# The end of a decoder layer: the last columns in two groups of 256, their squares on VectorE, scalings and transfers shared out anew

## The chip, the cores and the metric

One core of one Trainium2 chip runs the whole layer. The metric is the device time of one execution in microseconds (us), the median over several runs. Engines are named as the profile names them: PE is TensorE (PEld its weight loads), DVE is VectorE, ACT is ScalarE, POOL is GpSimd, and SP (SPq) is SyncE, whose queue starts the transfers.

## The reference

`reference()` is one layer of a decoder with 256 tokens of width 1024: a block attention and a gated recurrence merged, a cross-attention, a SwiGLU feed-forward part, and a final RMSNorm. Only its end matters here:

```python
hn = rmsnorm(h, norm_ffn_g[l])
gu = hn @ w_ffn_in[l]
h = h + (jax.nn.silu(gu[..., :FFN_HIDDEN]) * gu[..., FFN_HIDDEN:]) @ w_ffn_out[l]
return rmsnorm(h, final_norm_g)     # h * rsqrt(mean(h * h, -1) + 1e-6) * gain, in float32
```

The result is a float32 matrix of 256 x 1024.

## The kernel before

All weights are streamed from HBM in units of 128 x 2048 floats, in a fixed order (`ORDER`). Each unit is split into a high and a low part (`hi`, `lo`, lines 181 and 185), and each product of two matrices takes three matmuls: high by high, high by low, low by high (`mm3t`, lines 225 to 227). Tokens lie on the partitions in two groups of 128, `t` = 0 and 1; the 1024 output columns lie in two groups of 512, `c` = 0 and 1.

The feed-forward part walks over 11 blocks of 256 hidden columns. `ffn_in` forms a block, `gate` and `turn_hid` bring it into the form `hid` that the next product needs, and `ffn_out(o)` (lines 1074 to 1088) adds block `o` times its weights into four accumulators `acc[t, c]`, each a whole PSUM bank of 128 x 512 floats. The matmuls of the last block, `ffn_out(10)`, are the last work of PE. They run in the order `(t, c)` = (0,0), (0,1), (1,0), (1,1), six of 512 columns to each accumulator.

Behind them stands the end of the kernel (lines 1106 to 1124), called the tail here. For each `(t, c)`, `add_h` (lines 882 to 888) adds the accumulator to the residual `H` on DVE and squares the sum on ACT, whose accumulator gives the row sums `ssq3`. The product `hg3` of `H` and the final gain is formed on POOL for `t` = 0 and on DVE for `t` = 1 (line 1113). Then `s` adds the two sums of squares (line 1115), `rstd_of` forms mean plus EPS on DVE (line 274) and raises it to the power -1/2 on POOL (line 276). Last, `hg3` is multiplied by that factor, columns 0 to 511 on ACT (line 1121), columns 512 to 1023 on DVE (line 1123), and each quarter of the output goes out as a transfer of its own from SP's queue (line 1124).

The order of PE's instructions is the program's. The order in the queues of the other engines is laid out by the framework when the program is built, by its own estimate of when each instruction becomes ready. So a queue's order may differ from the program's: in the trace, DVE's `s` of `t` = 0 (629.38 us) stands behind the addition of (1,0) (628.77 us), which comes later in the text. Waits between engines are also set by the framework, from the regions that instructions read and write.

Of the kernel before, what the change touches and what calls it, by code (L numbers as in the profile page):

```python
# [10 lines left out]
F32 = mybir.dt.float32  # L11
F32R = mybir.dt.float32r
I32 = mybir.dt.int32
AF = mybir.ActivationFunctionType
ALU = mybir.AluOpType
# [3 lines left out]
S, D, NK = 256, 1024, 8  # L19
# [5 lines left out]
EPS = 1e-6  # L25
# [86 lines left out]
def build(tc, A, out):  # L112
    nc = tc.nc
    V, SC, G, PE, SY = nc.vector, nc.scalar, nc.gpsimd, nc.tensor, nc.sync
    with ExitStack() as ctx:
        def pool(name, bufs, **k):
            return ctx.enter_context(tc.tile_pool(name=name, bufs=bufs, **k))

        cp = pool("cp", 1)
# [7 lines left out]
        def big(tag, name, shape=(128, 8, 256), dt=F32):  # L127
            return bp.tile(list(shape), dt, name=name, tag=tag)
# [4 lines left out]
        def t2b(name, shape=(128, 512)):  # L133
            return tb.tile(list(shape), F32, name=name, tag="tb")

        def small(name, shape):
            return sp.tile([128] + list(shape), F32, name=name)

        def bank(name, shape=(128, 512)):
            return sm.tile(list(shape), F32, name=name, tag="sm")  # L140
# [5 lines left out]
        nhalf = cp.tile([128, 4], F32, name="nhalf")  # L146
        ident = cst[:, C_ID:C_ID + 128]
        H = big("B0", "H", (128, 2, 1024))
# [43 lines left out]
        def nxt(lead=LEAD):  # L192
            i = at[0]
            at[0] += 1
            while made[0] <= min(i + lead, len(ORDER) - 1):
                run(prep())
            return ready.pop(i)
# [26 lines left out]
        def mm3t(ps, xh, xl, h, l, first, last):  # L224
            PE.matmul(ps, xh, h, start=first, stop=False)  # L225
            PE.matmul(ps, xh, l, start=False, stop=False)  # L226
            PE.matmul(ps, xl, h, start=False, stop=last)  # L227

        def by_k(w, k):
            return tuple(t.rearrange("p (k c) -> p k c", k=k) for t in w)  # L230
# [41 lines left out]
        def rstd_of(ssq, name, n=2, mult=1.0 / D, eps=EPS):  # L272
            v = small("v_", [n])
            V.tensor_scalar(v, ssq, mult, eps, op0=ALU.mult, op1=ALU.add)
            r = cp.tile([128, n], F32, name="r_" + name)
            G.tensor_tensor(r, v, nhalf[:, :n], op=ALU.pow)
            return r
# [146 lines left out]
        for i in range(9):  # L424
            if i < 8:
                c, k = i // 4, i % 4
# [4 lines left out]
            if i > 0:  # L431
                c, k = (i - 1) // 4, (i - 1) % 4
                for t in range(2):
                    PE.matmul(pss[c][t], Xh[:, k, t * 128:(t + 1) * 128], ws[c][1][:, k], start=False, stop=False)
        w = by_k(nxt(), 4)
# [13 lines left out]
        w = by_k(nxt(), 4)  # L449
# [431 lines left out]
        def add_h(t, c, ps, scale, ssq):  # L881
            d = H[:, t, c * 512:(c + 1) * 512]
            if scale is None:
                V.tensor_tensor(d, ps, d, op=ALU.add)
            else:
                V.scalar_tensor_tensor(d, ps, scale, d, op0=ALU.mult, op1=ALU.add)
            j = t2b("hjunk")
            SC.activation(j, d, AF.Square, accum_out=ssq[:, t, c:c + 1])
# [128 lines left out]
        gfin = big("B5", "gfin", (128, 1024))  # L1017
# [29 lines left out]
        ring = ("B3", "B4", "B7", "B8", "B9", "B14")  # L1047
        X2 = (h2h, h2l)
        hid, acc, two, psi, hm = {}, {}, {}, {}, {}
# [9 lines left out]
        def turn_hid(o):  # L1059
            bk = mm.tile([128, 2, 256], F32, name="hidT", tag="mm")  # L1060
            for t in range(2):
                u = hm.pop((o, t))
                for j in range(2):
                    PE.transpose(bk[:, j, t * 128:(t + 1) * 128], u[:, j * 128:(j + 1) * 128], ident)
            hd = big(ring[o % 6], "hid", (128, 2, 2, 256), F32R)
            split(bk, hd[:, 0], hd[:, 1])
            hid[o] = hd
# [6 lines left out]
        def ffn_out(o):  # L1074
            w = by_k(nxt(), 2)
            last = o == NF // 2 - 1
            for t in range(2):
                ts = slice(t * 128, (t + 1) * 128)
                for c in range(2):
                    if (t, c) not in acc:  # L1080
                        acc[t, c] = bank("acc")
                    cs = slice(c * 512, (c + 1) * 512)
                    for k in range(2):
                        hh, hl = hid[o][:, 0, k], hid[o][:, 1, k]
                        mm3t(acc[t, c], hh[:, ts], hl[:, ts], w[0][:, k, cs], w[1][:, k, cs],
                             o == 0 and k == 0, last and k == 1)
                if o == NF // 2 - 2 and t == 0:
                    turn_hid(o + 1)

        for u in ORDER[at[0]:]:  # L1090
            if u[0] == "O":
                ffn_out(u[1])
                continue
            _, o, kh = u
            w = by_k(nxt(), 4)
            for t in range(2):
                ffn_in(o, kh, t, w)
                if (o, kh, t) == (0, 0, 0):
                    turn_h2(1, 1)
                    two["r"] = rstd2(ssq2, "h2")  # L1100
                if kh == 1:
                    gate(o, t)
            if kh == 0 and o:
                turn_hid(o - 1)

        ssq3 = cp.tile([128, 2, 2], F32, name="ssq3")
        hg3, rs = {}, {}
        for t in range(2):
            for c in range(2):
                a = slice(c * 512, (c + 1) * 512)  # L1110
                add_h(t, c, acc[t, c], None, ssq3)
                hg3[t, c] = big(ring[2 * t + c], "hg3", (128, 512))
                (G if (t, c) in ((0, 0), (0, 1)) else V).tensor_tensor(hg3[t, c], H[:, t, a], gfin[:, a], op=ALU.mult)
            s = small("s3", [1])
            V.tensor_tensor(s, ssq3[:, t, 0:1], ssq3[:, t, 1:2], op=ALU.add)
            rs[t] = rstd_of(s, "f%d" % t, n=1)
        for t in range(2):
            for c in range(2):
                a = slice(c * 512, (c + 1) * 512)
                if c == 0:  # L1120
                    SC.activation(H[:, t, a], hg3[t, c], AF.Copy, scale=rs[t])
                else:
                    V.tensor_scalar(H[:, t, a], hg3[t, c], rs[t], None, op0=ALU.mult)
                SY.dma_start(out[t * 128:(t + 1) * 128, a], H[:, t, a])


# [38 lines left out]
```

## Time and profile before

| what | value |
|---|---|
| median of 3 runs | 638.32 us (638.22 to 639.06) |
| the profiled execution's own time | 639.19 us |
| its span, first to last instruction | 637.4 us |
| busy: PE, DVE, ACT, POOL | 619.7, 380.0, 326.2, 367.1 us |
| granted TensorE clock, mean | 0.991 |
| chain of waits that ended last | PE 89% |

The span is what the profile shows instruction by instruction; 1.79 us of the profiled execution's own time lie outside it. The window from the first addition of the tail to the end of the span reaches from 626.05 to 637.4 us.

### The profile page before, as it was taken

What the parts mean: (1) busy time and instruction counts of PE and PEld (TensorE: products, weight loads), DVE (VectorE), ACT (ScalarE), POOL (GpSimd) and SP (SyncE); (2) the same over time, 40 slices, a digit from 0 to 9 for tenths busy, and PEclk for the clock granted to TensorE, in tenths of its full rate; (3) what the DMA queues carried; (4) which work ended last, traced back from release to release, by engine and by line L of the source; (5) the groups of instructions that cost most, each with busy time, mean ns of one, the idle gap of its engine ahead of it and who ended that gap; (6) DMA issues with size and microseconds to landing.
All of it is one profiled execution on the core that took longest, in us unless ns stands there. A gap on an engine that the chain in (4) does not pass through costs nothing.

```text
span 637.4 us, 8670 instructions
## 1 busy us (share of the span) xinstructions
PE 619.7 (97%) x3262; PEld 521.4 (82%) x3262; DVE 380.0 (60%) x649; ACT 326.2 (51%) x513; POOL 367.1 (58%) x289
## 2 busy tenths in 40 slices
PE   7996999999999999999999999999999999999995
PEld 6784888888887777778889999888888888888884
DVE  6462677888857777685646446664444444444433
ACT  6683544433457667673455444554444444444433
POOL 0588555455644564446857767656566555666552
PEclk9998999999999999999999999999999999999998
DMA  8760633443533333535544454462355544455511
GB/s 270 297 240 20 249 147 133 164 171 137 190 132 134 133 132 133 198 135 197 196 159 173 174 192 165 173 250 77 132 193 199 192 176 174 189 194 198 198 66 66
DMA packets 17177, 107.52 MB, mean 169 GB/s; under 512 B 2160, under 2 KB 2544, under 8 KB 4720
## 3 DMA queue, kind: packets, MB, share of 16 engines
q1 hardware_dynamic: 17136, 106.98, 46.6%
q8 instruction: 25, 0.41, 0.3%
q14 instruction: 16, 0.13, 0.1%
HBM read 105.92 MB, written 1.05 MB: 168 GB/s over the span
## 4 chain that ended last, share of the span: by engine, by line
PE 89%; POOL 5%; DMA 3%; issue 1%; SPq 1%; ACT 0%; DVE 0%; POOLq 0%; DVEq 0%; ACTq 0%
PE pst L225 13%; PE pst L226 13%; PE pst L227 13%; PE psi L225 6%; PE psi L227 6%; PE psi L226 6%; PE acc L227 3%; PE acc L226 3%; PE acc L225 3%; PE psf L220 2%; PE psf L221 2%; PE psf L222 2%; PE lp L582 2%; DMA H<-xtok 2%; PE pso L225 1%; PE pso L227 1%
## 5 line engine op out<-in xcount | busy, mean ns | idle before, releaser
L185 POOL TENSOR_TENSOR lo<-raw,hi 128x448 fp32r<-128x448 f32 x174 | 271.0, 1572 | 190.0 <-ACT hi L181 183.3
L181 ACT ACTIVATE hi<-raw 128x1024 fp32r<-128x1024 f32 (+1 forms) x194 | 196.3, 1037 | 199.7 <-PE pst L227 62.7
L185 DVE TENSOR_TENSOR lo<-raw,hi 128x576 fp32r<-128x576 f32 (+2 forms) x194 | 194.1, 1005 | 143.5 <-ACT hi L181 126.7
L226 PE MATMUL pst<-lo,Xh 128*128 128x512 f32 x256 | 100.7, 393 | 6.1 <-POOL lo L185 6.1
L225 PE MATMUL pst<-hi,Xh 128*128 128x512 f32 x256 | 103.8, 405 | 0.0
L227 PE MATMUL pst<-hi,Xl 128*128 128x512 f32 x256 | 100.6, 393 | 0.0
L225 PE MATMUL psi<-hi,h2h 128*128 128x512 f32 x176 | 69.6, 396 | 0.0
L227 PE MATMUL psi<-hi,h2l 128*128 128x512 f32 x176 | 68.7, 390 | 0.0
L226 PE MATMUL psi<-lo,h2h 128*128 128x512 f32 x176 | 68.6, 390 | 0.0
L226 PEld LDWEIGHTS pst<-lo,Xh 128*128 128x128 f32 x256 | 48.7, 190 | 15.7 <-POOL lo L185 6.5
L227 PEld LDWEIGHTS pst<-hi,Xl 128*128 128x128 f32 x256 | 48.5, 189 | 10.3
L225 PEld LDWEIGHTS pst<-hi,Xh 128*128 128x128 f32 x256 | 48.6, 190 | 10.1 <-issue 0.7
L227 PEld LDWEIGHTS psi<-hi,h2l 128*128 128x128 f32 x176 | 33.1, 188 | 7.1
L226 PEld LDWEIGHTS psi<-lo,h2h 128*128 128x128 f32 x176 | 33.1, 188 | 6.5
L225 PEld LDWEIGHTS psi<-hi,h2h 128*128 128x128 f32 x176 | 33.1, 188 | 6.5
L225 PE MATMUL acc<-hi,hid 128*128 128x512 f32 x88 | 34.3, 390 | 0.0
L226 PE MATMUL acc<-lo,hid 128*128 128x512 f32 x88 | 34.3, 389 | 0.0
L227 PE MATMUL acc<-hi,hid 128*128 128x512 f32 x88 | 34.3, 389 | 0.0
L1056 DVE SCALAR_TENSOR_TENSOR fu<-psi,r_h,fg 128x256 f32<-128x256 f32 x22 | 10.6, 483 | 26.1 <-ACT fg L1054 26.1
L1054 ACT ACTIVATE fg<-psi,r_h 128x256 f32<-128x256 f32 x22 | 10.5, 475 | 29.9 <-PE psi L227 29.9
L227 PEld LDWEIGHTS acc<-hi,hid 128*128 128x128 f32 x88 | 16.5, 188 | 3.4
L225 PEld LDWEIGHTS acc<-hi,hid 128*128 128x128 f32 x88 | 16.5, 188 | 3.4
(338 smaller groups left out, 1172.1 us busy)
## 6 DMA issues: line engine op xcount, KB each, us to landing
raw<-w SPq DMA_DIRECT2D x95, 1024.0 KB, 4.8
raw<-w SPq DMA_DIRECT2D x8, 256.0 KB, 5.8
H<-xtok SPq DMA_DIRECT2D x1, 1024.0 KB, 10.2
mraw<-mT SPq DMA_DIRECT2D x1, 1024.0 KB, 7.0
out<-H SPq DMA_DIRECT2D x4, 256.0 KB, 2.2
xraw<-xT SPq DMA_DIRECT2D x3, 256.0 KB, 5.9
gfin<-gfin SPq DMA_DIRECT2D x1, 512.0 KB, 4.9
cst<-cst SPq DMA_DIRECT2D x1, 272.0 KB, 8.9
```

What stands on the lines that cost most here:

```text
L181: SC.activation(hi[:, a], raw[:, a], AF.Copy)
L185: eng.tensor_tensor(lo[:, b], raw[:, b], hi[:, b].bitcast(F32), op=ALU.subtract)
L220: PE.matmul(ps, lh, rh, start=first, stop=False)
L221: PE.matmul(ps, lh, rl, start=False, stop=False)
L222: PE.matmul(ps, ll, rh, start=False, stop=last)
L225: PE.matmul(ps, xh, h, start=first, stop=False)
L226: PE.matmul(ps, xh, l, start=False, stop=False)
L227: PE.matmul(ps, xl, h, start=False, stop=last)
L582: PE.matmul(ps[:, j], KS[:, a0 + j], QQ[:, a0 + j], start=True, stop=True)
L1054: SC.activation(g, ps[:, 0:256], AF.Silu, scale=r)
L1056: V.scalar_tensor_tensor(u, ps[:, 256:512], r, g, op0=ALU.mult, op1=ALU.mult)
```

## The change

In `ffn_out(10)` alone, the accumulators of the second column group, `acc[0, 1]` and `acc[1, 1]`, are filled in two groups of 256 columns, one after the other, in the same bank. Each group takes six matmuls of 256 columns in place of one group's six of 512.

The tail then walks over three column cuts, 0 to 511, 512 to 767 and 768 to 1023. Each has its addition on DVE. The squares of the first two are summed on ACT as before (the factor 1/32 before the square gives the division by 1024). `pre` adds these two sums and EPS on DVE, and the squares of the third cut are summed on DVE by one `tensor_tensor_reduce` that starts from `pre`, so its result `v` is the mean plus EPS. POOL raises `v` to -1/2 as before. `hg3` is one tile of 128 x 1024 for each `t`; its product is on POOL for the first two cuts of `t` = 0 and on DVE for the rest. The scalings are shared out as: `t` = 0, columns 0 to 511 on POOL, 512 to 1023 on DVE; `t` = 1, columns 0 to 383 on ACT, 384 to 1023 on DVE. There are still four transfers, one behind each scaling, from SP's queue but for the one behind ACT's scaling, which ACT's own queue starts.

```diff
@@ ffn_out @@
-                    cs = slice(c * 512, (c + 1) * 512)
-                    for k in range(2):
-                        hh, hl = hid[o][:, 0, k], hid[o][:, 1, k]
-                        mm3t(acc[t, c], hh[:, ts], hl[:, ts], w[0][:, k, cs], w[1][:, k, cs],
-                             o == 0 and k == 0, last and k == 1)
+                    for u, v in ((0, 256), (256, 512)) if last and c == 1 else ((0, 512),):
+                        cs = slice(c * 512 + u, c * 512 + v)
+                        for k in range(2):
+                            hh, hl = hid[o][:, 0, k], hid[o][:, 1, k]
+                            mm3t(acc[t, c][:, u:v], hh[:, ts], hl[:, ts], w[0][:, k, cs], w[1][:, k, cs],
+                                 o == 0 and k == 0, last and k == 1 and v == 512)
@@ tail @@
-        ssq3 = cp.tile([128, 2, 2], F32, name="ssq3")
+        ssq3 = cp.tile([128, 2, 3], F32, name="ssq3")
+        CUTS = ((0, 512), (512, 768), (768, 1024))
         hg3, rs = {}, {}
         for t in range(2):
-            for c in range(2):
-                a = slice(c * 512, (c + 1) * 512)
-                add_h(t, c, acc[t, c], None, ssq3)
-                hg3[t, c] = big(ring[2 * t + c], "hg3", (128, 512))
-                (G if (t, c) in ((0, 0), (0, 1)) else V).tensor_tensor(hg3[t, c], H[:, t, a], gfin[:, a], op=ALU.mult)
-            s = small("s3", [1])
-            V.tensor_tensor(s, ssq3[:, t, 0:1], ssq3[:, t, 1:2], op=ALU.add)
-            rs[t] = rstd_of(s, "f%d" % t, n=1)
+            hg3[t] = big(ring[t], "hg3", (128, 1024))
+            for i, (u, w) in enumerate(CUTS):
+                d, a = H[:, t, u:w], acc[t, u // 512][:, u % 512:u % 512 + w - u]
+                V.tensor_tensor(d, a, d, op=ALU.add)
+                j = t2b("hjunk")[:, :w - u]
+                if i < 2:
+                    SC.activation(j, d, AF.Square, scale=1.0 / 32.0, accum_out=ssq3[:, t, i:i + 1])
+                else:
+                    pre, v = small("pre", [1]), small("v3", [1])
+                    V.tensor_scalar(pre, ssq3[:, t, 0:1], ssq3[:, t, 1:2], EPS, op0=ALU.add, op1=ALU.add)
+                    V.tensor_tensor_reduce(out=j, in0=d, in1=d, op0=ALU.mult, op1=ALU.add, scale=1.0 / D,
+                                           scalar=pre, accum_out=v)
+                    rs[t] = cp.tile([128, 1], F32, name="r_f%d" % t)
+                    G.tensor_tensor(rs[t], v, nhalf[:, :1], op=ALU.pow)
+                (G if t == 0 and i < 2 else V).tensor_tensor(hg3[t][:, u:w], d, gfin[:, u:w], op=ALU.mult)
         for t in range(2):
-            for c in range(2):
-                a = slice(c * 512, (c + 1) * 512)
-                if c == 0:
-                    SC.activation(H[:, t, a], hg3[t, c], AF.Copy, scale=rs[t])
-                else:
-                    V.tensor_scalar(H[:, t, a], hg3[t, c], rs[t], None, op0=ALU.mult)
-                SY.dma_start(out[t * 128:(t + 1) * 128, a], H[:, t, a])
+            rows_out = out[t * 128:(t + 1) * 128]
+            for eng, u, w in (((G, 0, 512), (V, 512, 1024)), ((SC, 0, 384), (V, 384, 1024)))[t]:
+                if eng is SC:
+                    SC.activation(H[:, t, u:w], hg3[t][:, u:w], AF.Copy, scale=rs[t])
+                else:
+                    eng.tensor_scalar(H[:, t, u:w], hg3[t][:, u:w], rs[t], None, op0=ALU.mult)
+                (SC if eng is SC else SY).dma_start(rows_out[:, u:w], H[:, t, u:w])
```

## Prediction

> **What bounds the kernel now.** I read the page's chain first: PE holds nearly all of it, so almost the whole span is a row of matmuls that the change leaves alone. Then I read the chain of waits over the end of the span, to see where PE lets go.
>
> ```profile
> PE 89%; POOL 5%; DMA 3%; issue 1%; SPq 1%; ACT 0%; DVE 0%; POOLq 0%; DVEq 0%; ACTq 0%
> ...
> 628.51 0.24 PE acc L227
> ...
> 628.77 0.69 DVE H L884
> ...
> 633.29 0.72 ACT H L1121
> ```
>
> From 628.77 on the chain runs through DVE, POOL and ACT. The change can only touch what lies behind about 627 us: a tail of some 10 us, of which PE covers the first part. So I took the timeline of these microseconds (start, duration, engine, line).
>
> ```profile
> 627.41 0.69 DVE L884 TENSOR_TENSOR H<-acc,H 128x512 f32<-128x512 f32 x1 [0.67 <-PE acc L227]
> ...
> 628.35 0.39 PE L227 MATMUL acc<-hi,hid 128*128 128x512 f32 x1
> ...
> 629.50 0.69 DVE L1113 TENSOR_TENSOR hg<-H,gfin 128x512 f32<-128x512 f32 x1
> ...
> 629.71 0.39 PE L227 MATMUL acc<-hi,hid 128*128 128x512 f32 x1
> ...
> 630.11 0.14 DVE L274 TENSOR_SCALAR v__5431<-s 128x1 f32<-128x1 f32 x1
> 630.17 0.68 DVE L884 TENSOR_TENSOR H<-acc,H 128x512 f32<-128x512 f32 x1
> 630.34 0.55 POOL L276 TENSOR_TENSOR r_f<-v__5431,nhalf 128x1 f32<-128x1 f32 x1 [0.85 <-DVE v__5431 L274]
> 630.92 0.72 ACT L1121 ACTIVATE H<-hg,r_f 128x512 f32<-128x512 f32 x1 [0.63 <-POOL r_f L276]
> 630.92 0.49 DVE L1123 TENSOR_SCALAR H<-hg,r_f 128x512 f32<-128x512 f32 x1
> ...
> 631.54 0.61 ACT L888 ACTIVATE hjunk<-H 128x512 f32<-128x512 f32 x1
> ...
> 632.06 0.19 ACT L888 ACTIVATION_READ_ACCUMULATOR hjunk<-H 128x1 f32 x1
> 632.28 0.16 DVE L1115 TENSOR_TENSOR s<-ssq 128x1 f32<-128x1 f32 x1 [0.28 <-ACT hjunk L888]
> 632.48 0.15 DVE L274 TENSOR_SCALAR v__5447<-s 128x1 f32<-128x1 f32 x1
> 632.71 0.55 POOL L276 TENSOR_TENSOR r_f<-v__5447,nhalf 128x1 f32<-128x1 f32 x1 [1.83 <-DVE v__5447 L274]
> 633.29 0.72 ACT L1121 ACTIVATE H<-hg,r_f 128x512 f32<-128x512 f32 x1 [1.04 <-POOL r_f L276]
> 633.30 0.49 DVE L1123 TENSOR_SCALAR H<-hg,r_f 128x512 f32<-128x512 f32 x1 [0.67 <-POOL r_f L276]
> ```
>
> The last matmul ends at 629.71 + 0.39 = 630.10. The addition ends at 630.85, but ACT starts its squares only at 631.54, because it took the scaling of `t` = 0 first (630.92): 0.6 us lost in a queue. The sum is there at 632.25, two small DVE steps take it to 632.63, POOL's power to 633.26, the scalings to 633.79 (DVE) and 634.01 (ACT). What follows is the last pair of transfers:
>
> ```profile
> L1124 SPq DMA_DIRECT2D out<-H x2: 332/382/431, 633.8 to 634.2; - x2
> ...
> DMA to landing us min/median/max: 2.0/2.2/2.3
> ...
> 634.60:636.40 1.80, 0.00 (x0) 0.00 (x0) 0.00 (x0) 0.00 (x0) 0.00 (x0) 0.50 0.75 291
> ```
>
> The second starts at 634.2, when SP is through with the first, and lands at about 636.5. The two move data from 634.6 to 636.4 (DMA share 0.75, 291 GB/s), and the span ends 1.0 us later, at 637.4.
>
> **PE's part of the change.** Twelve accumulations of 512 columns become 24 of 256. The pitch at 512 is (629.71 - 628.35) / 6 = 0.227 us. For 256 columns with the same weight loads I take the attention scores:
>
> ```profile
> 408.53 0.28 PE L225 MATMUL xs<-kxh,qxh 128*128 128x256 f32 x1
> ...
> 409.13 0.28 PE L227 MATMUL xs<-kxh,qxl 128*128 128x256 f32 x1
> ```
>
> Five steps in 0.60 us: a pitch of 0.12. A bank takes 12 x 0.12 = 1.44 us where it took 6 x 0.227 = 1.36, so two banks end PE 0.16 us later, at 630.26. The halved groups are nearly free.
>
> **Does a half come out sooner?** The intention can only be that `H`'s columns 512 to 767 are added while PE fills 768 to 1023. Both lie in one bank, and all matmuls stand before the additions in the text. The trace has one such case: the bank `as` of the block attention, whose columns 0 to 127 are filled first and read first by DVE (line 737), the others behind.
>
> ```profile
> 234.41 0.93 PE L730 MATMUL as<-kT,qT 64*128 64x128 f32 x8
> ...
> 235.36 0.29 DVE L737 CUSTOM_DVE_ANT_0 ap<-as,cst 128x128 f32<-128x128 f32 x1 [1.27 <-PE as L730]
> ...
> 266.28 0.93 PE L730 MATMUL as<-kT,qT 64*128 64x128 f32 x8
> ...
> 267.24 0.29 DVE L737 CUSTOM_DVE_ANT_0 ap<-as,cst 128x128 f32<-128x128 f32 x1 [2.07 <-PE as L730]
> ```
> ```profile
> L730 PE MATMUL as<-kT,qT x4: 375/377/378, 234.7 to 235.0; 64*128 64x256 f32 x4
> ```
>
> The second fence is the tile's PE work in the window 235.1 to 235.2: only matmuls of the 256-column part still run, so the first 128 columns are done. DVE had nothing to do for 1.27 us, yet it starts at 235.36, right behind the last matmul of all (234.41 + 0.93). At 267.24 it is the same (266.28 + 0.93 = 267.21). Two of two: a read waits for the whole bank. I therefore take it that both additions of `acc[1, 1]` wait until 630.26, and the split itself brings nothing.
>
> **The tail after.** Prices for what is new or smaller:
>
> ```profile
> L737 DVE CUSTOM_DVE_ANT_0 ap<-as,cst 128x256 f32<-128x256 f32 x16 | 6.7, 416 | 0.0
> L737 DVE DVE_READ_ACCUMULATOR2_ANT amx<- 128x1 f32 x32 | 2.6, 81 | 0.0
> L267 DVE TENSOR_TENSOR oal<-ao,oah 128x256 fp32r<-128x256 f32 x8 | 3.3, 416 | 0.0
> L405 ACT ACTIVATE QQ<-QP 128x256 f32<-128x256 f32 x4 | 1.7, 432 | 0.0
> L824 POOL TENSOR_TENSOR tat<-tat,tbt 128x512 f32<-128x512 f32 x4 | 5.2, 1290 | 1.7 <-DVE tat L823 1.7
> L940 POOL TENSOR_TENSOR qxl<-kx,qxh 128x512 fp32r<-128x512 f32 x4 | 7.4, 1860 | 0.0
> ```
>
> A 256-column DVE step takes 0.42, and the next starts 0.08 sooner than its end (629.50 + 0.69 against 630.11), so a queue of them goes at 0.34, of 512 columns at 0.61. The multiply-and-sum is not in the trace; its sister of line 737 costs 0.42 + 0.08, a full 512-column pass 0.69 would be the upper end; I take 0.50. POOL's scaling of 512 columns lies between its power on one column (0.55) and 1.86; I take 1.29, the plainest row of that width. DVE's scaling of 640 columns lies between 0.49 and 0.49 x 640/512 = 0.61, ACT's of 384 between 0.43 and 0.72: 0.61 each.
>
> `t` = 0: the addition of 627.41 moves to 627.49, the next to 627.83. ACT's squares of 512 to 767 are there at 627.93 + 0.43 + 0.10 = 628.46, `pre` at 628.65, the multiply-and-sum at 629.2, POOL's power at 629.85. POOL then scales until 631.2 (at most 631.8); `t` = 1's power stands behind it, but isn't wanted before 632.2, so this costs nothing, and would only if the scaling took over 2.3 us. DVE goes on with the addition of (1,0), ready at 628.85 but queued until 629.2, then its 512-column product until 630.4.
>
> `t` = 1: PE is done at 630.26, DVE free at 630.4 (0.15 lost). Addition of 512 to 767, its product, addition of 768 to 1023: 3 x 0.34 + 0.08, until 631.5. ACT's squares of the first run beside them: 630.85 + 0.43 + 0.10 = 631.4, so they are hidden. `pre` ends at 631.65, the multiply-and-sum at 632.15, the power (0.08 + 0.55, as from 632.63 to 633.26) at 632.78, both scalings at 633.4. The last product (0.34) hides behind the power. Before, the same point was 633.79 and 634.01.
>
> Both transfers then start at about 633.4, on two queues, where SP started one at 633.8 and one at 634.2. If the pair is bound by moving its 512 KB, which took 1.8 us, only the first start counts: 0.4 gained. If each lands 2.3 behind its own start, the second counts: 0.8. A transfer that ACT starts is not in the trace, and I price it as SP's. The Trainium skill (DMA: Bandwidth & Descriptors, Issuing engines are not separate DMA queues) says that starting from several engines saves just the sequencer's time for the start; by it the whole 0.4 us of SP's second start is gained, and the sum would be 0.8. The share of 0.75 in the window above says that the transfers share one pipe already, which speaks for the lower end. I take the middle, **0.6 us**.
>
> Against the profiled execution: 639.19 - 0.6 = 638.6. That execution lies 0.87 above the median; the same step from the median gives 638.32 - 0.6 = **637.7 us**. A measurement of this kernel can tell about 0.2%, 1.28 us, from no change, so I forecast no change that can be told.
>
> **Rivals.**
>
> A. *DVE's queue.* Where the framework lays DVE's scaling of `t` = 0 (0.49 - 0.08) ahead of `t` = 1's additions, the chain is 0.4 later; with the 0.34 of `t` = 0's last product as well, 0.75. For it: the queue of before took just this scaling in front of a product (630.92). Against: there the addition of 630.17 went first. It gives 0.2 slower to 0.4 faster: 637.9 to 638.5, say 638.2.
>
> B. *The halves do come apart.* Columns 512 to 767 are then ready at 630.26 - 0.72 = 629.54. If also DVE adds (1,0) ahead of `t` = 0's multiply-and-sum, at 628.85, ACT has its two squares by 630.85, the second addition runs at 630.28, `pre` ends at 631.05, the power at 632.25, the scalings at 632.9: a gain of 0.9 to 1.3 us, and of 1.6 if the pair lands in 2.0: 636.7 to 637.4. Against it stand the two waits on `as`. The Trainium skill (PSUM — Partial Sum Buffer, PSUM bank collisions raise a hardware error) has the rule to guard PSUM by bank and not by address; by that rule this rival has no chance.
>
> C. *Slower: ACT's queue.* The transfer that ACT starts goes over a queue that no row shows, and it is the last one. Where it shares the pipe badly, its price is that of transfers of this size among others:
>
> ```profile
> raw<-w SPq DMA_DIRECT2D x8, 256.0 KB, 5.8
> gv<-gv SPq DMA_DIRECT2D x1, 28.0 KB, 1.8
> ```
>
> At 5.8 us it lands at 639.2, 2.7 later than now: 641.0. It decides from 3.1 us on, and is slower by over 1.28 from 4.4. Against it: SP's own first transfer (`gv`) landed in 1.8, and at the end nothing else is under way.
>
> **How the numbers follow.** My case 0.45, A 0.22, B 0.25, C 0.08. Mine and A lie within 0.2%; of B about half lies beyond 1.28 us: faster 0.13, same 0.79, slower 0.08. My case alone reaches from 637.4 to 638.0; A and most of B widen it to 636.9 to 638.6; C is left out.
>
> **What would show it.** Right: 24 matmuls of 256 columns 0.12 apart; both last additions behind the last matmul; DVE's `tensor_tensor_reduce` of about 0.42 with POOL's power behind it; ACT's squares no longer behind a scaling; the scalings ending within 0.1 of each other at 633.4; two starts at once. Wrong: an addition of 256 columns while PE still fills that bank (B), DVE busy with `t` = 0 at 630.4 (A), POOL's scaling over 2.3 us, or a landing above 3 us (C).

## The result and the profile after

| | before | after |
|---|---|---|
| median | 639.3 us (13 runs) | 640.07 us (13 runs) |
| ratio after to before, 95% interval | | 1.002 (1.0013 to 1.0028) |
| profiled execution: own time, span | 639.19, 637.4 us | 639.8, 637.8 us |
| DVE, POOL, ACT busy | 380.0, 367.1, 326.2 us | 382.4, 369.6, 324.9 us |

The change makes the kernel slower by about 1.3 us, where 0.6 us less was forecast. The median of before is also 1.0 us higher over 13 runs than over the three that the prediction started from, so the ratio is what counts.

The first addition of the tail stands anywhere from 625.26 to 626.62 us in the profiles of the fourteen kernels, so I count the tail from this addition (columns 0 to 511 of `t` = 0, when the first accumulator is full) to the end of the span: before 637.4 - 626.05 = 11.35 us, after 637.8 - 625.62 = 12.18 us. The tail alone is 0.83 us longer. The span is printed to 0.1 us, so a tail is good to about 0.05. VectorE's timeline of the changed kernel, from that addition on:

```profile
625.62 0.69 DVE L1115 TENSOR_TENSOR H<-acc,H 128x512 f32<-128x512 f32 x1 [2.79 <-PE acc L227]
627.05 0.76 DVE L1115 TENSOR_TENSOR H<-acc,H 128x256 f32<-128x256 f32 x2 [0.74 <-PE acc L227]
627.84 0.82 DVE L1126 TENSOR_TENSOR hg<-H,gfin 128x256 f32<-128x256 f32 x1
...
628.71 0.67 DVE L1115 TENSOR_TENSOR H<-acc,H 128x512 f32<-128x512 f32 x1
629.31 0.47 DVE L1122 CUSTOM_DVE_ANT_0 hjunk<-H,pre 128x256 f32<-128x256 f32 x1
...
629.71 0.68 DVE L1126 TENSOR_TENSOR hg<-H,gfin 128x512 f32<-128x512 f32 x1
630.31 0.74 DVE L1115 TENSOR_TENSOR H<-acc,H 128x256 f32<-128x256 f32 x2
630.98 0.41 DVE L1126 TENSOR_TENSOR hg<-H,gfin 128x256 f32<-128x256 f32 x1
...
631.43 0.70 DVE L1126 TENSOR_TENSOR hg<-H,gfin 128x256 f32<-128x256 f32 x1
632.06 0.47 DVE L1122 CUSTOM_DVE_ANT_0 hjunk<-H,pre 128x256 f32<-128x256 f32 x1
...
632.46 0.56 DVE L1133 TENSOR_SCALAR H<-hg,r_f 128x512 f32<-128x512 f32 x1
633.48 0.55 DVE L1133 TENSOR_SCALAR H<-hg,r_f 128x640 f32<-128x640 f32 x1 [0.46 <-POOL r_f L1125]
```

From 627.05 VectorE hardly stops until 633.02. The same form of product takes 0.41 once (630.98) and 0.82 and 0.70 at other places. The slow one at 627.84, of `t` = 0's third cut, runs beside POOL's two products and holds up what follows: the accumulator of (1,0) is full at 628.01 + 0.39 = 628.40, its addition starts at 628.71.

```profile
626.39 1.99 POOL L1126 TENSOR_TENSOR hg<-H,gfin 128x512 f32<-128x512 f32 x2 [9.42 <-DVE H L1115]
```
```profile
628.01 0.39 PE L227 MATMUL acc<-hi,hid 128*128 128x512 f32 x1
```

The last matmul ends at 629.83, and `t` = 1's last two additions start 0.48 us later. That the multiply-and-sum of `t` = 0 (629.31) stands behind the addition of (1,0) makes no difference to them, but puts `t` = 0's own sum back by 0.6. Another product (631.43) stands ahead of `t` = 1's multiply-and-sum. POOL, and its place in the chain of waits:

```profile
629.87 0.93 POOL L1125 TENSOR_TENSOR r_f<-v,nhalf 128x1 f32<-128x1 f32 x1 [1.48 <-DVE v L1122]
630.90 1.85 POOL L1133 TENSOR_SCALAR H<-hg,r_f 128x512 f32<-128x512 f32 x1
632.72 0.73 POOL L1125 TENSOR_TENSOR r_f<-v,nhalf 128x1 f32<-128x1 f32 x1
```
```profile
629.87 0.94 POOL r_f L1125
630.81 0.09 issue
630.90 1.85 POOL H L1133
632.74 0.71 POOLq L1170
633.46 0.02 issue
633.48 0.62 ACT H L1131
```

POOL's scaling takes 1.85 us, its powers 0.93 and 0.73 where before had 0.55 twice. The transfers follow (SP's row holds its three starts; the line below ACT's is the window 633.7 to 636.5, its last two numbers the share of the DMA engines and GB/s; the second fence has the shortest, median and longest of SP's starts in ns, and when the first and the last of them begin):

```profile
632.77 1.62 SPq L1134 DMA_DIRECT2D out<-H  x3
634.13 0.37 ACTq L1134 DMA_DIRECT2D out<-H  x1
633.70:636.50 2.80, 0.00 (x0) 0.00 (x0) 0.33 (x1) 0.40 (x1) 0.00 (x0) 0.50 0.95 367
```
```profile
L1134 SPq DMA_DIRECT2D out<-H x3: 332/347/423, 632.8 to 634.1; - x3
```

`t` = 0's first transfer starts at 632.77, 7.15 us behind the first addition, where before it started at 631.66, 5.61 behind. `t` = 1's first transfer is the third of SP's starts and begins at 632.77 + 1.62 - 0.33 = 634.06, 8.44 behind, where before it started at 633.81, 7.76 behind. All four transfers, 1 MB, then run in one piece at a share of 0.95.

### The profile page after: what moved, and what is told of

Its sections match the earlier page's. It is cut to its first block, busy times and chain, and to the rows that moved or that the text cites. A ratio compares the mean times of both kernels' runs of the same rounds, so it can differ in the third digit from the quotient of the medians.

```text
span 637.8 us, 8700 instructions
## 1 busy us (share of the span) xinstructions
PE 620.1 (97%) x3274; PEld 522.2 (82%) x3274; DVE 382.4 (60%) x655; ACT 324.9 (51%) x512; POOL 369.6 (58%) x290
## 4 chain that ended last, share of the span: by engine, by line
PE 88%; POOL 6%; DMA 2%; issue 1%; SPq 1%; ACT 0%; DVE 0%; POOLq 0%; DVEq 0%; ACTq 0%
PE pst L225 13%; PE pst L226 13%; PE pst L227 13%; PE psi L225 6%; PE psi L227 6%; PE psi L226 6%; PE acc L227 3%; PE acc L226 3%; PE acc L225 3%; PE psf L221 2%; PE psf L220 2%; PE psf L222 2%; PE lp L582 2%; DMA H<-xtok 2%; PE pso L225 1%; PE pso L227 1%
## 5 line engine op out<-in xcount | busy, mean ns | idle before, releaser
L225 PE MATMUL acc<-hi,hid 128*128 128x512 f32 (+1 forms) x92 | 35.0, 381 | 0.0
L226 PE MATMUL acc<-lo,hid 128*128 128x512 f32 (+1 forms) x92 | 35.0, 380 | 0.0
L227 PE MATMUL acc<-hi,hid 128*128 128x512 f32 (+1 forms) x92 | 34.9, 380 | 0.0
L1056 DVE SCALAR_TENSOR_TENSOR fu<-psi,r_h,fg 128x256 f32<-128x256 f32 x22 | 10.6, 484 | 26.0 <-ACT fg L1054 26.0
L225 PEld LDWEIGHTS acc<-hi,hid 128*128 128x128 f32 x92 | 17.3, 188 | 3.3
L226 PEld LDWEIGHTS acc<-lo,hid 128*128 128x128 f32 x92 | 17.3, 188 | 3.3
```

The source lines that it names most:

```text
L1056: V.scalar_tensor_tensor(u, ps[:, 256:512], r, g, op0=ALU.mult, op1=ALU.mult)
```

## The experiments

Three theories. P: POOL is too slow for its new place, so `t` = 0's transfers and `t` = 1's power come late. Q: VectorE has too much work ahead of `t` = 1's sum. A: the transfer from ScalarE's queue costs time. All results, with the starts of the first transfer of each `t` counted from the first addition, like the tail:

| kernel | `t` = 0's first transfer, us | `t` = 1's first transfer, us | tail, us | ratio to before (interval) |
|---|---|---|---|---|
| before | 5.61 | 7.76 | 11.35 | |
| after | 7.15 | 8.44 | 12.18 | 1.002 (1.0013 to 1.0028) |
| e1 | 6.29 | 8.06 | 11.72 | 1.0008 (0.9999 to 1.0017) |
| e2 | 7.14 | 8.49 | 12.12 | 1.0013 (1.0004 to 1.0022) |
| e3 | 7.15 | 8.44 | 12.21 | 1.0011 (1.0002 to 1.002) |
| e4 | 6.89 | 8.28 | 11.94 | 1.0009 (1.0 to 1.0018) |
| o1 | 5.57 | 8.24 | 11.91 | 1.0009 (0.9998 to 1.0019) |
| o2 | 5.86 | 7.69 | 11.32 | 1.0003 (0.9994 to 1.0011) |
| o3 | 5.64 | 7.65 | 11.32 | 0.9997 (0.9986 to 1.0009) |
| b1 | 5.38 | 7.62 | 11.21 | 0.9993 (0.9984 to 1.0001) |
| p1 | 7.33 | 8.40 | 12.34 | 1.0013 (1.0004 to 1.0022) |
| p2 | 5.39 | 8.91 | 12.48 | 1.002 (1.001 to 1.0029) |
| m1 | 6.21 | 7.77 | 11.44 | 1.0006 (0.9997 to 1.0015) |
| m2 | 5.63 | 7.15 | 10.77 | 1.0 (0.999 to 1.0011) |

The intervals of the times are wider than most steps between kernels. Over the 13 kernels the tail's difference to before and the time's go together (correlation 0.88, slope 0.88), so the tail, whose steps repeat to a few hundredths, is what I read.

**e1: `t` = 0's scaling from POOL back to ScalarE**, in the idle time behind its last squares; both of `t` = 0's transfers stay on SP.

```diff
-            for eng, u, w in (((G, 0, 512), (V, 512, 1024)), ...
+            for eng, u, w in (((SC, 0, 512), (V, 512, 1024)), ...
```

> Theory P (POOL is too slow for a place in the tail: its scaling of t = 0 took 1.85 us, stood in front of t = 1's power and held back t = 0's transfers by a microsecond): with that scaling in ACT's idle time, t = 1's power starts 0.1 us behind the sum and takes 0.55 in place of 0.73, t = 0's transfers start near 632.0 in place of 632.8 us and no longer meet those of t = 1; the tail from the last matmul to the end of the span shrinks from 7.97 us by 0.4 to 0.7. Theory Q (VectorE has too many steps ahead of t = 1's sum) and theory A (ScalarE's queue for a transfer): nothing but the 0.2 of the power, t = 1's sum ends as late as before and the last landing stays within 0.2 us.

The tail shrinks by 0.46, as theory P said, but `t` = 1's own transfers also start 0.38 sooner: the power no longer stands behind POOL's scaling, and with POOL idle the product of line 1126 goes back from 0.70 to 0.41:

```profile
631.80 0.41 DVE L1126 TENSOR_TENSOR hg<-H,gfin 128x256 f32<-128x256 f32 x1
...
632.54 0.47 DVE L1133 TENSOR_SCALAR H<-hg,r_f 128x512 f32<-128x512 f32 x1
```
```profile
632.69 0.73 POOL L1125 TENSOR_TENSOR r_f<-v,nhalf 128x1 f32<-128x1 f32 x1 [1.53 <-DVE v L1122]
```

But the power keeps its 0.73: it is not POOL's own queue that slows it, but VectorE's scaling (632.54) beside it. That part of the expectation missed. In all fourteen tails the power takes 0.55 to 0.57 where VectorE is idle or adds out of PSUM, and 0.69 to 0.99 where its products or scalings run beside it. Nearly half of the loss is left.

**e2: all transfers from SP.**

```diff
-                (SC if eng is SC else SY).dma_start(rows_out[:, u:w], H[:, t, u:w])
+                SY.dma_start(rows_out[:, u:w], H[:, t, u:w])
```

> Theory A (the transfer from ScalarE's queue costs time, in its landing of 2.7 us or outside the span): 0.3 to 0.8 us faster than the changed kernel. Theories P and Q: the two last starts are behind each other again, one 0.3 to 0.4 us later, and the end comes 0 to 0.4 us later; time outside the span is unchanged.

Tail -0.06, hardly more than the printed span can tell: theory A falls. The second queue gains nothing either: the last start comes 0.4 us behind the one before it again, and the end does not move.

**e3: one group of 512 again, three cuts in the tail.**

```diff
-                    for u, v in ((0, 256), (256, 512)) if last and c == 1 else ((0, 512),):
+                    for u, v in ((0, 512),):
```

> The last accumulators are filled in one group of 512 again, the tail keeps its three cuts. If the halves of a bank never came apart (both additions wait for the last matmul): PE ends 0.16 us sooner against the same work, the tail keeps its 7.97 us, the time goes down by 0.1 to 0.2 us. If the split did bring the first addition forward: up to 0.5 us slower.

Tail +0.03, no change that the printed span can tell. PE's 0.16 us are really gone, but nothing waits for them: `t` = 1's additions start 0.65 us behind the last matmul (630.69 against 630.04) at the pace of VectorE's queue.

**e4: the third cut's squares on ScalarE.**

```diff
-                    V.tensor_tensor_reduce(out=j, in0=d, in1=d, ..., scalar=pre, accum_out=v)
+                    SC.activation(j, d, AF.Square, scale=1.0 / 32.0, accum_out=ssq3[:, t, 2:3])
+                    V.tensor_tensor(v, pre, ssq3[:, t, 2:3], op=ALU.add)
```

> The squares of the third cut go back to ScalarE, with a one-column addition to pre on VectorE in place of the multiply-and-sum. Theory Q: the sum of t = 1 no longer waits behind VectorE's products; the sum is ready at the last addition's end + 0.42 + 0.10 + 0.2, near 631.9 where the multiply-and-sum ended at 632.54, and the tail is 0.3 to 0.6 us shorter. Theory P: POOL's power still waits for the scaling until 632.75, so nothing is gained beyond 0.1 us.

Tail -0.24, less than theory Q wanted and more than P. The sum is there 2.79 us behind the last matmul (after: 2.71), no sooner, because VectorE's new order puts `t` = 0's scaling ahead of `t` = 1's additions. What it gains is the power, 0.57 in place of 0.73, which now finds POOL free and VectorE done.

One number runs through the fourteen kernels of the table. From the start of `t` = 1's first transfer to the end of the span there are 3.57 to 3.77 us in thirteen of them, and 3.94 in p1. It holds whether the DMA engines stand idle between the transfers of `t` = 0 and `t` = 1 (before, o1, o2, o3, b1, p2) or run in one piece (after, e2, e3, e4), and whether the second start of the pair comes 0.4 behind the first or at once. So the end follows the start of `t` = 1's first transfer.

The start of `t` = 0's first transfer is a second limit. Where it is late, the tail is that start plus nearly a constant: after 12.18 - 7.15 = 5.03, e2 4.98, e3 5.06, e4 5.05, p1 5.01, the time that four transfers in one piece need. In the changed kernel the two limits meet: 8.44 plus the 3.57 to 3.67 of the kernels with a gap gives 12.01 to 12.11, the late start of `t` = 0 gives 12.1 to 12.2. So POOL's late handing out of `t` = 0 adds at most 0.2 us; o1 below, where it is gone and `t` = 1's start is not, says the same. The chain of waits names POOL's scaling, but puts ScalarE's scaling last and shows no DMA.

**o1: VectorE's order by hand, nothing else.** Each step is traced in the order wanted and pinned there.

```diff
+        add(0, 0); gain(0, 0, G); add(0, 1); gain(0, 1, G); add(0, 2); total(0)
+        add(1, 0); gain(0, 2, V); scaled(0, G, 0, 512); scaled(0, V, 512, 1024)
+        add(1, 1); add(1, 2); gain(1, 0, V); total(1); gain(1, 1, V); gain(1, 2, V)
+        scaled(1, SC, 0, 384); scaled(1, V, 384, 1024)
```

(`total` is `pre`, the multiply-and-sum and the power; `gain` is a product with the final gain.)

> The changed kernel with its steps and engines, but VectorE's order written by hand: t = 0's multiply-and-sum ahead of the addition of (1,0), t = 1's multiply-and-sum ahead of the products of its last two cuts, t = 0's scaling ahead of t = 1's last additions. Theory Q (VectorE's queue became the bound of the tail): t = 1's sum ends 0.4 to 0.6 us sooner, t = 0's transfers start near 631.5, and the tail from the last matmul to the end of the span is 7.3 to 7.6 us where the changed kernel has 7.97. Theory P (POOL alone): the power of t = 1 still comes behind a scaling of 1.85 us, so the tail stays within 0.2 of 7.97.

```profile
629.71 0.72 DVE L1140 TENSOR_SCALAR H<-hg,r_f 128x512 f32<-128x512 f32 x1
```
```profile
628.75 0.55 POOL L1134 TENSOR_TENSOR r_f<-v,nhalf 128x1 f32<-128x1 f32 x1 [0.50 <-DVE v L1131]
629.39 1.64 POOL L1140 TENSOR_SCALAR H<-hg,r_f 128x512 f32<-128x512 f32 x1
632.43 0.69 POOL L1134 TENSOR_TENSOR r_f<-v,nhalf 128x1 f32<-128x1 f32 x1 [1.39 <-DVE v L1131]
```

Tail -0.27; counted from the last matmul 7.70, which misses the 7.3 to 7.6. `t` = 0's first transfer is early again (5.57 in place of 7.15), although POOL still scales it: its power starts 0.99 sooner (3.26 behind the first addition, after 4.25), takes 0.55 in place of 0.93, and the scaling 1.64 in place of 1.85. So most of POOL's lateness came from VectorE's queue, and 1.58 us of it gone shorten the tail by no more than 0.27. `t` = 1 is the bound: its sum is ready only 0.07 us sooner than in the changed kernel, because `t` = 0's scaling, now ahead of its additions, takes 0.72 beside POOL. Its transfers start 0.20 sooner.

**o2: order by hand, and `t` = 0's scalings both on ScalarE.**

```diff
+        add(1, 0); add(1, 1); add(1, 2); gain(0, 2, V)
+        scaled(0, SC, 0, 512); scaled(0, SC, 512, 1024)
+        total(1); gain(1, 0, V); gain(1, 1, V); gain(1, 2, V); ...
```

> The same multiply-and-sum and split, but t = 0's scalings both on ScalarE behind its last squares, VectorE's order by hand with t = 1's additions right behind each other. If VectorE's and POOL's work explains the loss, the tail is 6.7 to 7.1 us, below the 7.30 of the kernel before, and the time 0.2 to 0.6 us below it. On VectorE the addition of columns 512 to 767 of t = 1 sits idle until the last matmul of the bank ends, 0.3 to 0.5 us, if the wait is for the whole bank; if it is for the half, it starts at once.

Tail 11.32 (7.11 from the last matmul, just over the range), level with before: the order by hand and `t` = 0's scalings on ScalarE together take back the whole 0.83. The time does not show the 0.2 to 0.6 us below before that were expected (1.0003, 0.9994 to 1.0011). VectorE waits for the bank, idle 0.47 us, until the last matmul ends at 630.19; and POOL's power takes 0.94 beside three products.

```profile
630.23 0.75 DVE L1116 TENSOR_TENSOR H<-acc,H 128x256 f32<-128x256 f32 x2 [0.47 <-PE acc L227]
```
```profile
632.05 0.94 POOL L1134 TENSOR_TENSOR r_f<-v,nhalf 128x1 f32<-128x1 f32 x1 [2.27 <-DVE v L1131]
```

**o3: as o2, the last block's product for columns 768 to 1023 of `t` = 1 in a bank of its own.**

```diff
+                            own = last and t == 1 and u == 256
+                            mm3t(acc["own"][:, :256] if own else acc[t, c][:, u:v], ...)
...
+        keep(V.tensor_tensor(H[:, 1, 768:], acc["own"][:, :256], H[:, 1, 768:], op=ALU.add))
```

> As the kernel with ScalarE's scalings and the order by hand, but the last block's product for columns 768 to 1023 of t = 1 goes to a bank of its own, and a fourth addition (0.34 us) brings it in. If a read waits for a whole bank: VectorE's addition of columns 512 to 767 now starts while PE still fills the other bank, 0.3 to 0.5 us before the last matmul ends, with no idle time ahead of it, and the tail changes by -0.3 to 0.1 us against that kernel (the head start is spent on the added addition). If it waits for all of PE: the addition starts at the last matmul as before and the tail is 0.35 longer.

The three additions of `t` = 1 out of the old banks now run in one go from 628.57 to 629.92, over the end of the last matmul (629.41 + 0.28 = 629.69), with no idle time ahead. So it is the bank that a read waits for, and not all of PE; each bank is one tile here, so the two are not told apart. The head start pays for the added addition: tail as in o2.

```profile
628.57 1.35 DVE L1120 TENSOR_TENSOR H<-acc,H 128x512 f32<-128x512 f32 x3
```
```profile
629.41 0.28 PE L227 MATMUL own<-hi,hid 128*128 128x256 f32 x1
```

**b1: the kernel before, ScalarE's scaling of `t` = 0 pinned behind the squares of (1,1).**

```diff
-                    SC.activation(H[:, t, a], hg3[t, c], AF.Copy, scale=rs[t])
+                    tc.keep_in_program_order(SC.activation(H[:, t, a], hg3[t, c], AF.Copy, scale=rs[t]))
```

> The kernel before, with one instruction moved: ScalarE's scaling of t = 0 behind the squares of (1,1). If the 0.6 us that the squares lost in that queue are on the path: the squares start near 630.9, t = 1's sum and both last scalings come 0.6 sooner, the tail is 6.7 in place of 7.30 us, and the time goes down by about 0.6 us, 0.1%. If t = 0's transfers, then later by 0.6, collide with t = 1's: 0.2 to 0.4.

Tail 11.21, only -0.14. The squares start at once, but `s` then stands behind VectorE's product, so the scalings come 0.37 us sooner and not 0.6. `t` = 1's first transfer starts only 0.14 sooner: it starts right behind ScalarE's scaling (633.26 + 0.72 = 633.98), where in the kernel before VectorE's came first (633.30 + 0.49).

**p1: the kernel before with POOL scaling `t` = 0's first half.**

```diff
+                    if t == 0:
+                        G.tensor_scalar(H[:, t, a], hg3[t, c], rs[t], None, op0=ALU.mult)
```

> The kernel before with one part of the change alone: t = 0's columns 0 to 511 scaled on POOL. Counted from the first addition of the tail to the end of the span, the kernel before has 11.35 us, the changed one 12.18. ScalarE's squares of (1,1) are rid of the scaling ahead of them (0.6 us), so t = 1's sum is ready near 632.2 on before's clock. Theory P (POOL's scaling takes 1.6 to 1.9 us in the tail and t = 1's power stands behind it): that power starts only at 632.6 to 632.8, takes 0.55 to 0.75, t = 0's transfer starts near 632.7 in place of 631.66 and meets t = 1's; the tail is 11.4 to 11.8. If POOL's scaling takes 1.29 as forecast: the power starts at 632.3, the tail is 11.0 to 11.2.

```profile
631.49 2.38 POOL L1122 TENSOR_SCALAR H<-hg,r_f 128x512 f32<-128x512 f32 x1
633.84 0.57 POOL L276 TENSOR_TENSOR r_f<-v__5447,nhalf 128x1 f32<-128x1 f32 x1
```

2.38 us, more than either version allowed, and the power waits 0.7 us for it (its input was there at 633.18). This part alone makes the tail 12.34, beyond both ranges and longer than the whole change does. Here alone `t` = 0's late transfers hold up the end clearly: `t` = 1's first start stands 3.94 ahead of it.

**p2: the kernel before with the squares of columns 512 to 1023 on VectorE.**

```diff
+                    V.tensor_scalar(pre, ssq3[:, t, 0:1], EPS, None, op0=ALU.add)
+                    V.tensor_tensor_reduce(out=j, in0=d, in1=d, ..., scalar=pre, accum_out=v)
```

> The kernel before with one other part alone: the squares of columns 512 to 1023 summed on VectorE from a start value, no split, no new sharing. VectorE gets about 0.7 us of work more for each t, and its queue as laid out puts t = 0's scaling and a product ahead of the addition of (1,1) and another product ahead of t = 1's multiply-and-sum. Theory Q (VectorE's queue is the bound): that addition starts 0.5 to 0.7 us behind the last matmul, t = 1's scalings start near 633.6 where before has 633.3, the tail is 11.3 to 11.7 although ScalarE's stall of 0.6 us is gone. If the multiply-and-sum were worth its idea: scalings near 632.4, tail 10.5.

```profile
628.77 1.82 DVE L1119 CUSTOM_DVE_ANT_0 hjunk<-H,pre 128x512 f32<-128x512 f32 x1
...
633.60 0.74 DVE L1119 CUSTOM_DVE_ANT_0 hjunk<-H,pre 128x512 f32<-128x512 f32 x1
```
```profile
627.39 2.66 POOL L1124 TENSOR_TENSOR hg<-H,gfin 128x512 f32<-128x512 f32 x2 [9.42 <-DVE H L1112]
```

Tail 12.48, in place of 11.3 to 11.7. The order did what was expected, and a cost came on top that no theory had: the same instruction takes 0.74 alone and 1.82 beside POOL's two products, until half a microsecond after they end (630.05).

**m1 and m2: a version without these faults.** Own bank as in o3; ScalarE scales `t` = 0; VectorE's last pass multiplies by factor and gain in one step, so most products fall away.

```diff
 (m1)
+        add(0, 2); gain(0, 2, G); total(0); add(1, 0); gain(1, 0, G); add(1, 1); add(1, 2)
...
+        keep(V.scalar_tensor_tensor(d, d, rs[1], gfin[:, 512:], op0=ALU.mult, op1=ALU.mult))
 (m2: behind total(0), so that POOL's products stand beside additions out of PSUM)
+        add(0, 2); total(0); add(1, 0); keep(G.tensor_tensor(hg3[1][:, :384], ...)); gain(0, 2, G)
```

> What the runs so far point to: the last 256 columns of t = 1 in a bank of their own, four of the gain products on POOL, where nothing waits for them, VectorE left idle while POOL raises to the power, and VectorE's last scaling taking the gain along in one pass. If VectorE's queue and the slowing of POOL's power beside it (0.94 where it is 0.55 alone) are the rest of the loss: the power of t = 1 takes 0.55 to 0.6, t = 1's two transfers start 0.4 to 0.7 us sooner than in the own-bank kernel, the tail is 10.6 to 11.0 us, and the time 0.3 to 0.8 us (0.05 to 0.12%) below the kernel before. If POOL's products run beside VectorE's work and get slow (1.9 for 512 columns), the power comes late and the tail is about 11.3, as in the own-bank kernel.

> As m1, but POOL's products only stand beside VectorE's additions out of PSUM: the product of t = 0's third cut and a product of 384 columns for t = 1 come behind t = 0's power, and VectorE's last pass takes 640 columns with their gain. Theory R (VectorE's steps with both inputs in SBUF and POOL's products hold each other up, steps with one input in PSUM do not): t = 0's multiply-and-sum takes 0.5 again where m1 had 1.06, VectorE's additions keep 0.41 and 0.69 beside POOL, t = 1's power ends near 6.4 us after the first addition of the tail (7.0 in m1), and the tail is 10.6 to 10.9 us against 11.35 of the kernel before, the time 0.05 to 0.13% below it. If the additions slow down too: no better than m1's 11.4.

```profile
627.95 1.06 DVE L1135 CUSTOM_DVE_ANT_0 hjunk<-H,pre 128x256 f32<-128x256 f32 x1
```
```profile
629.11 0.48 DVE L1135 CUSTOM_DVE_ANT_0 hjunk<-H,pre 128x256 f32<-128x256 f32 x1
...
629.52 1.35 DVE L1120 TENSOR_TENSOR H<-acc,H 128x512 f32<-128x512 f32 x3
```
```profile
630.29 1.00 POOL L1155 TENSOR_TENSOR hg<-H,gfin 128x384 f32<-128x384 f32 x1
631.25 0.73 POOL L1129 TENSOR_TENSOR hg<-H,gfin 128x256 f32<-128x256 f32 x1
632.34 0.56 POOL L1138 TENSOR_TENSOR r_f<-v,nhalf 128x1 f32<-128x1 f32 x1 [0.36 <-DVE v L1135]
```

The first line is m1's, the rest m2's. In m1 POOL's product still met the multiply-and-sum (1.06), and the tail stayed at 11.44, not in the 10.6 to 11.0 hoped for. In m2 it takes 0.48, the additions beside POOL's product (630.29) keep their pace, the power takes 0.56, and the tail is 10.77, 0.58 shorter than before and in the range expected. The time does not show it: 1.0 (0.999 to 1.0011), so no version here is measured faster than the kernel before.

## Why the prediction was wrong

- **PE's part: right.** First addition to last matmul grows from 4.05 to 4.21 us, the 0.16 forecast. e3 shows that it lies on no path.
- **A read waits for its bank: right**, from two waits in the trace of before; o2 and o3 show both sides. The split brings nothing, and rival B falls.
- **VectorE's prices: right alone** (0.47 + 0.07 for the multiply-and-sum, 0.41, 0.55). **Its queue: wrong, and this is the step that failed most.** `t` = 1's sum was to be there at 632.15, 6.10 behind the first addition; it was there at 632.54, 6.92 behind, 0.82 late. "DVE free at 630.4", 0.15 behind the last matmul, was 0.48: the product of `t` = 0's third cut was left out of the sum, and took 0.82. "The last product hides behind the power": the framework put it ahead of the multiply-and-sum, and it took 0.70. At 0.41 the first would have ended ahead of 628.40 and held up nothing, and the second would be 0.29 shorter; by this estimate about 0.6 of the 0.82 is slowing beside POOL, the rest the order.
- **Rival A** named VectorE's queue, at 0.4 to 0.75, but with `t` = 0's scaling as the step in the way. That one stands behind `t` = 1's sum here (632.46); only `t` = 0's last product came as it said.
- **Beside each other, VectorE and POOL slow down: not in the forecast at all**, though before's rows had a spread of 1.29 to 1.86 for POOL's 512 columns. I took it as a spread of POOL's own price.
- **POOL on `t` = 1's path: 0.28 mis-sized.** The power was priced at 0.63 with its wait; it waits 0.18, for POOL's scaling, and takes 0.73. With the 0.82 this is the whole delay of `t` = 1's first transfer, 8.44 in place of 633.4 - 626.05 = 7.35.
- **POOL's scaling of 1.29: mis-sized**, 1.85 in the changed kernel and 2.38 in p1. That it costs nothing below 2.3 us was wrong too: `t` = 0's power ended 5.18 behind the first addition in place of 3.80, so already 1.85 reached into `t` = 1's power. What `t` = 0's own transfers lose was not asked. They start 1.54 us later than before, and not 0.46 sooner as by the forecast's 631.2, and are now as late as `t` = 1's.
- **Two starts at once: nothing.** Of the 0.4 to 0.8, 0.4 stood for a first start at 633.4 in place of 633.8, which came later instead; the rest stood for the second start. Both did start at 634.1. The rule of the Trainium skill (DMA: Bandwidth & Descriptors, Issuing engines are not separate DMA queues), that only the time of the start is saved, is an upper bound here: e2 gives it back and loses nothing. Rival C did not happen (landing 2.7).

So most of the loss lies on the path of `t` = 1, whose first transfer starts 0.68 us later than before. That of `t` = 0 had slack before, when it would have ended at 5.61 + 5.03 = 10.64, and has none after; the 0.15 that is left of the 0.83 may be its share, which is not shown. The sum of 0.83 us in the tail lies at the lower end of the interval of the time (0.0013 x 639); that the rest is more than the measurement's own scatter is not shown.

## What to carry to other kernels

Look for the one start that the end follows in every variant: here it is the first transfer of the last pair, 3.6 to 3.8 us ahead of the end, and what does not move it gains little. Sum the path of the earlier transfers too: one that comes late can become a second limit beside it. Do not take the step that the chain of waits names longest for the cause before a run has taken it away. Before moving work to another engine, ask which instructions of a third engine it will run beside, and look for rows of the same form with different durations: the spread is a price. And where a planner lays out a queue, an idea about which step is hidden needs the order pinned by hand.

## What the runs showed of the hardware

VectorE's steps with both inputs in SBUF and POOL's work hold each other up in many places: 0.74 and 1.82 us for the same 512 columns, 0.48 and 1.06 for 256, POOL's power 0.55 and 0.94; additions with one input in PSUM keep 0.41 and 0.69. The Trainium skill (SBUF — State Buffer, Who interferes with whom) states this: a VectorE instruction with two SBUF inputs contends with a GpSimd instruction that reads SBUF, one with at most one SBUF input does not, outside the modes that use both of VectorE's ports, and the shared ports are an exclusive lock. The traces agree for the products, the multiply-and-sums and the additions, and with a lock as far as p2's 1.82 goes, which ends 0.54 us behind POOL's products.

Two things the runs leave open. VectorE's scaling, one matrix and a one-column factor, is held up too (0.72 in o1, 0.47 in e1) and holds up the power (0.73 in e1); no run shows whether the factor or the mode does it. And who waits changes: a product takes its 0.41 at 630.98 while POOL's scaling runs (630.90 to 632.75), and one of 512 columns its 0.68 in p1 (631.83) while POOL's takes 2.38.
